# Moving the split weights' buffers in SBUF relative to the activations: a one-layer decoder on one core

## Chip, cores and metric

The kernel runs on one core of a Trainium2 chip. The metric is the device time of one execution in microseconds (us); the median of 3 runs is given, and a profile of one further execution.

## What is computed

One decoder layer over 512 tokens of width 1024, in float32. It has three parts, each followed by a layer norm of the sum with its input: a parallel mixer (chunked gMLP and stick-breaking attention behind one input projection, merged by gates, and an output projection), cross-attention into 256 memory tokens, and a mixture of 64 SwiGLU experts with 8 experts a token plus a shared one. Cut to what takes most of the time:

```python
proj = x @ w_in + b_in                               # 1024 x 7168
x = layer_norm(ALPHA * x + merged @ w_out)           # after gMLP and attention
m = softmax(q @ k.T) @ v @ w_mem_o                   # 4 heads, 256 memory tokens
moe = swiglu(x, w_sh_gate, w_sh_up, w_sh_down) + \
    routed_experts(x, idx, gate_w, w_exp_gate, w_exp_up, w_exp_down)   # 64 experts
```

## The kernel before, in words

**Products in three parts.** Each float32 operand of a large product is split into hi (rounded to fp32r) and lo (the rest, also fp32r). ScalarE writes hi and VectorE writes lo (`split`, line 80). A product is then three matmuls (`mm3`, lines 83 to 85): first operand's hi with the second's hi, hi with lo, lo with hi. The first argument pair of `mm3` holds the weights that are loaded into the array (128 x 128), the second is streamed through it (256 or 512 columns). While one matmul streams its operand, the weights of the next are loaded.

**Where the split weights lie.** `wpieces` (line 87) brings weight matrices from HBM through a ring of 1 MB slots and splits them in pieces of 1024 elements a partition into the pool `wq`. There, hi and lo have a tag each (`h` and `l`) with four buffers of 4096 bytes, so there are four pairs that are used in turn. The same pool takes the pieces of the shared expert's down projection (`shared`, line 637), of each expert's gate and up weights (`block_up`, line 712, two tiles for each half) and of its down weights (`down_split`, line 737, two tiles). Each pair serves two rows of K at 512 columns, which is six matmuls in the expert stage.

**Addresses.** A pool's tiles lie one behind the other in SBUF, and pools on the left side lie behind the pools opened earlier; some pools are placed from the right end. Worked out from the tiles' sizes, nearly all operands of TensorE start at 224 bytes modulo 512, and so do their slices: the eight buffers of `wq`, the activations `xTh`/`xTl`, the experts' `xb`, `hth` and `htl`, the attention's operands, `Mh`/`Ml`. Others are: the memory queries `QTh`/`QTl` and probabilities `PTh`/`PTl` at 64; the memory keys and `Vl` (right side) at 480; the shared expert's `HTh`/`HTl` at 32; the router's weights, whose slices are 256 bytes long, by turns at 224 and 480.

**Order of the work.** First the memory keys and values; then four pairs of attention heads, each with four projections (`proj_feat` streams the activations past the weights, `proj_tok` streams the weights past the activations); then the gMLP's v and u blocks, the gate, the output projection, memory attention, router, shared expert. The experts come last, 65 blocks (64 experts and one for an expert with over 128 tokens) of 128 rows each. In a block TensorE does 12 matmuls of the first half of gate and up, two transposes for the block before it, 12 of the second half, eight transposes of the gathered rows of the next block, and 12 of the down projection of the block before. Both halves and the down projection have 512 columns, with weights streamed past the activations. POOL gathers rows and adds results by indirect DMA; SP issues the weight loads.

```python
    def split(hi, lo, src):
        return nc.scalar.copy(hi, src), nc.vector.tensor_sub(lo, src, hi.bitcast(FT))

    def mm3(ps, s, m, start, stop):
        nc.tensor.matmul(ps, s[0], m[0], start=start, stop=False)
        nc.tensor.matmul(ps, s[0], m[1], start=False, stop=False)
        nc.tensor.matmul(ps, s[1], m[0], start=False, stop=stop)
```

```python
        for k0 in range(4 * half, 4 * half + 4, 2):
            hi = wq.tile([128, 2, 2, EH], FR, name="ehi", tag="h")
            lo = wq.tile([128, 2, 2, EH], FR, name="elo", tag="l")
            split(hi, lo, wgu[half][:, :, k0 - 4 * half:k0 - 4 * half + 2].rearrange("p g k n -> p k g n"))
            for j in range(2):
                k = k0 + j
                m = (hi[:, j].rearrange("p g n -> p (g n)"), lo[:, j].rearrange("p g n -> p (g n)"))
                mm3(hp, (x[:, k, 0], x[:, k, 1]), m, k == 0, k == KC - 1)
```

Of the kernel before, what the change touches and what calls it, by code (L numbers as in the profile page):

```python
# [10 lines left out]
FR = mybir.dt.float32r  # L11
# [8 lines left out]
D = 1024  # L20
# [6 lines left out]
EH = 256  # L27
# [11 lines left out]
def decoder_layer(ctx: ExitStack, tc: tile.TileContext, I, out, dbg=None):  # L39
# [4 lines left out]
    wq = ctx.enter_context(tc.tile_pool(name="wq", bufs=4, reuse_waits="tile"))  # L44
# [17 lines left out]
    def accps(i=None):  # L62
        return pp.tile([128, 512], FT, name="acc", tag="a", bufs=4)
# [9 lines left out]
    mhalf = cp.tile([128, 1], FT, name="mhalf")  # L73
    nc.vector.memset(mhalf, -0.5)

    def bcast(src, n):
        return bass.AP(tensor=src.tensor, offset=src.offset, ap=[[0, 128], [1, n]])

# [8 lines that stand above are left out]
    def wpieces(view, K, N):  # L87

        per = min(K, 2048 // N)
        kk = max(1, 1024 // N)  # L90
        raw = []
        for k0 in range(0, K, per):
            raw.append(ring.tile([128, per, N]))
            nc.sync.dma_start(raw[-1], view[:, k0:k0 + per])
        for k0, r in zip(range(0, K, per), raw):
            for k1 in range(0, per, kk):
                hi = wq.tile([128, kk, N], FR, name="whi", tag="h")
                lo = wq.tile([128, kk, N], FR, name="wlo", tag="l")
                split(hi, lo, r[:, k1:k1 + kk])
                for j in range(kk):  # L100
                    yield k0 + k1 + j, (hi[:, j], lo[:, j])

    def resident(view, K, N):
        return [w for _, w in wpieces(view, K, N)]

    def ln_load(g, b):
        gt, bt = row_pair("ln", "t01")
        nc.sync.dma_start(gt, bcast(g, D))
        nc.sync.dma_start(bt, bcast(b, D))
        return gt, bt  # L110
# [68 lines left out]
    with tc.tile_pool(name="pk", bufs=1, reuse_waits="tile") as pk:  # L179
# [8 lines left out]
        for c in range(2):  # L188
            on_act, on_dve = transpose_split(mth, mtl, mts[c], c)
        wk = wpieces(w_kv[:, :, 0:512], KC, 512)  # L190
        with tc.issue_after(on_act.ins), tc.issue_after(on_dve.ins):
            w0 = next(wk)
# [431 lines left out]
    for c in range(NCH):  # L624
        o = pps[:, c * NE:(c + 1) * NE]
# [11 lines left out]
    def shared():  # L637
        with tc.tile_pool(name="sh", bufs=1, reuse_waits="tile") as sh:
            HTh = sh.tile([128, 2, T], FR, name="HTh")
            HTl = sh.tile([128, 2, T], FR, name="HTl")  # L640
            wsg = resident(I["w_sh_gate"][0].rearrange("(p k) n -> p k n", k=KC), KC, EH)
            wsu = resident(I["w_sh_up"][0].rearrange("(p k) n -> p k n", k=KC), KC, EH)
            for hf in range(2):
                hs = slice(hf * 256, (hf + 1) * 256)
                for j in range(2):
                    js = slice(j * 128, (j + 1) * 128)
                    pg, pu = accps()[:, 0:256], accps()[:, 0:256]
                    for w, ps in ((wsg, pg), (wsu, pu)):
                        for k in range(KC):
                            mm3(ps, (w[k][0][:, js], w[k][1][:, js]), (xTh[:, k, hs], xTl[:, k, hs]),  # L650
                                k == 0, k == KC - 1)
                    SG = sh.tile([128, 256], FT, name="SG", tag="SG", bufs=2)
                    nc.scalar.activation(SG, pg, AF.Silu)
                    nc.vector.tensor_tensor(SG, SG, pu, op=OP.mult)
                    split(HTh[:, j, hs], HTl[:, j, hs], SG)
            stage = xp.tile([128, NCH, D], FT, name="stage", tag="xTh")
            wsd = ring.tile([128, 2, D])
            nc.sync.dma_start(wsd, I["w_sh_down"][0].rearrange("(k p) n -> p k n", p=128))
            for n0 in (0, 512):
                hi = wq.tile([128, 2, 512], FR, name="shi", tag="h")  # L660
                lo = wq.tile([128, 2, 512], FR, name="slo", tag="l")
                split(hi, lo, wsd[:, :, n0:n0 + 512])
                for c in range(NCH):
                    cs = slice(c * 128, (c + 1) * 128)
                    ps = accps()
                    for k in range(2):
                        mm3(ps, (HTh[:, k, cs], HTl[:, k, cs]), (hi[:, k], lo[:, k]), k == 0, k == 1)
                    nc.scalar.copy(stage[:, c, n0:n0 + 512], ps)
                    if n0:
                        nc.scalar.dma_start(accv[1][:, c], stage[:, c])  # L670
# [8 lines left out]
    for i in range(4):  # L679
        t = ea.tile([128, D], FT, name="xg%d" % i, tag="xg%d" % i, bufs=1)  # L680
# [31 lines left out]
    def block_up(wgu, slot, half, hp):  # L712

        x = late[1][:, slot]
        for k0 in range(4 * half, 4 * half + 4, 2):
            hi = wq.tile([128, 2, 2, EH], FR, name="ehi", tag="h")
            lo = wq.tile([128, 2, 2, EH], FR, name="elo", tag="l")
            split(hi, lo, wgu[half][:, :, k0 - 4 * half:k0 - 4 * half + 2].rearrange("p g k n -> p k g n"))
            for j in range(2):
                k = k0 + j  # L720
                m = (hi[:, j].rearrange("p g n -> p (g n)"), lo[:, j].rearrange("p g n -> p (g n)"))
                mm3(hp, (x[:, k, 0], x[:, k, 1]), m, k == 0, k == KC - 1)

    def block_h(hp, gate):
        hh = late[0].tile([128, EH], FT, name="hh", tag="hh")
        nc.scalar.activation(hh, hp[:, 0:EH], AF.Silu)
        mark[0] = nc.vector.scalar_tensor_tensor(hh, hp[:, EH:2 * EH], gate, hh, op0=OP.mult, op1=OP.mult)
        hv = hh.rearrange("t (p k) -> t k p", k=2)
        hps = zps().rearrange("p (k t) -> p k t", k=4)
        for k in range(2):  # L730
            nc.tensor.transpose(hps[:, k], hv[:, k], idf)  # L731
        hth = late[0].tile([128, 2, 128], FR, name="hth", tag="hth")
        htl = late[0].tile([128, 2, 128], FR, name="htl", tag="htl")
        split(hth, htl, hps[:, 0:2])
        return hth, htl

    def down_split(wd):
        w = []
        for k in range(2):
            hi = wq.tile([128, D], FR, name="dhi", tag="h")  # L740
            lo = wq.tile([128, D], FR, name="dlo", tag="l")
            split(hi, lo, wd[:, k])
            w.append((hi, lo))
        return w
# [134 lines left out]
    N = len(queue)  # L879
# [34 lines left out]
    for n in range(N):  # L914
# [5 lines left out]
        if prev:  # L920
            h = block_h(prev[1], prev[3])
# [97 lines left out]
```

## Time and profile before

| | |
|---|---|
| runs, median of 3 | 1233.82 us (1233.71 to 1235.24) |
| profiled execution | 1231.37 us |
| its span, first to last instruction | 1229.7 us |
| TensorE busy | 1172.8 us, 95% |
| VectorE busy | 958.5 us, 78% |
| ScalarE busy | 805.8 us, 66% |

A matmul's row tells when it starts and how long until its end; matmuls overlap, so what counts for a run of them is the distance from one start to the next. Lines 80 and 83 to 85 are those of helpers, so groups are told apart by their tiles: `ehi`, `elo` are the experts' gate and up weights, `dhi`, `dlo` their down weights, `whi`, `wlo` all weights that come through `wpieces`, `shi`, `slo` the shared expert's down weights. In a matmul's row the streamed operand and the weights stand behind the arrow, in either order.

### The profile page before, as it was taken

The page shows a single profiled execution, that of the slowest core. Times are in us where ns is not written, and L with a number is a line of the kernel's source. Part 1 is how long each engine was busy: PE and PEld are TensorE (multiplying, and loading weights), DVE is VectorE, ACT ScalarE, POOL GpSimd, SP SyncE. Part 2 cuts the span into 40 slices and gives each one's busy share as a digit, 9 for nine tenths or more (in the row PEclk, how much of TensorE's full clock was granted, in tenths as well). Part 3 has the DMA queues.
Part 4 walks back from the last instruction along what each step waited for, and adds up shares of the span by engine and source line. Part 5 has one row for each costly group of instructions (what it writes and reads, how often), then busy time and mean ns, then how long its engine had stood idle before and what let it go on. Part 6 is the DMA issues. An engine that isn't in the chain of part 4 may idle for free.

```text
span 1229.7 us, 17667 instructions
## 1 busy us (share of the span) xinstructions
PE 1172.8 (95%) x6301; PEld 992.5 (81%) x6301; DVE 958.5 (78%) x1427; ACT 805.8 (66%) x1198; POOL 267.4 (22%) x178
## 2 busy tenths in 40 slices
PE   7999999999999999989999999999999999999980
PEld 6887888878888889877888888888888888888860
DVE  6546556464745567885999999999999999999974
ACT  7444334343324346545888998989989899899971
POOL 2000000000200010121333433334433342334213
PEclk9999999999999999999999999999999999999995
DMA  9621322224333212477999999999999999999946
GB/s 342 215 85 57 107 69 70 69 69 141 117 106 135 103 62 102 171 265 268 360 393 376 385 397 370 379 368 394 389 383 389 383 385 371 368 374 340 388 115 150
DMA packets 102367, 307.73 MB, mean 250 GB/s; under 512 B 17358, under 2 KB 35334, under 8 KB 93446
## 3 DMA queue, kind: packets, MB, share of 16 engines
q1 hardware_dynamic: 78054, 259.05, 55.0%
q0 software_dynamic: 19296, 35.71, 12.1%
q10 hardware_dynamic: 4928, 11.83, 2.5%
q8 instruction: 50, 0.82, 0.3%
q14 instruction: 39, 0.32, 0.1%
HBM read 298.64 MB, written 42.47 MB: 277 GB/s over the span
## 4 chain that ended last, share of the span: by engine, by line
PE 77%; issue 6%; DVE 6%; DMA 5%; POOL 3%; ACT 1%; SPq 0%; POOLq 0%; DVEq 0%; ACTq 0%
PE acc L85 22%; PE acc L84 22%; PE acc L83 22%; PE trp L170 4%; DMA acc<-ys,idxs 2%; POOL acc L756 2%; DVE qq L283 2%; DMA ln<-in_ln_in_g_dram 1%; PE zp L84 1%; PE zp L85 1%; PE zp L83 1%; PE zp L731 1%; POOL xg L686 1%; DVE be L285 1%; DMA y<-acc 1%
## 5 line engine op out<-in xcount | busy, mean ns | idle before, releaser
L80 DVE TENSOR_TENSOR elo<-wraw,ehi 128x1024 fp32r<-128x1024 f32 x260 | 316.5, 1225 | 21.4 <-ACT ehi L80 20.4
L80 ACT CAST ehi<-wraw 128x1024 fp32r<-128x1024 f32 x260 | 274.1, 1055 | 44.4 <-PE acc L85 40.2
L83 PE MATMUL acc<-ehi,xb 128*128 128x512 f32 x520 | 208.1, 400 | 1.2 <-ACT xb L80 1.2
L85 PE MATMUL acc<-ehi,xb 128*128 128x512 f32 x520 | 205.9, 396 | 1.0 <-DVE xb L80 1.0
L84 PE MATMUL acc<-elo,xb 128*128 128x512 f32 x520 | 204.5, 393 | 0.0
L80 DVE TENSOR_TENSOR wlo<-wraw,whi 128x1024 fp32r<-128x1024 f32 x84 | 101.9, 1222 | 104.5 <-ACT whi L80 104.5
L80 ACT CAST whi<-wraw 128x1024 fp32r<-128x1024 f32 x84 | 87.5, 1050 | 127.4 <-PE acc L84 72.0
L756 POOL DMA_INDIRECT acc<-ys,idxs x65 | 130.9, 2014 | 170.4 <-ACT ys L755 145.0
L84 PE MATMUL acc<-xTl,whi 128*128 128x512 f32 (+1 forms) x448 | 162.0, 362 | 0.0
L83 PE MATMUL acc<-xTh,whi 128*128 128x512 f32 (+1 forms) x448 | 162.0, 362 | 0.0
L85 PE MATMUL acc<-xTh,wlo 128*128 128x512 f32 (+1 forms) x448 | 160.8, 360 | 0.0
L80 DVE TENSOR_TENSOR dlo<-wraw,dhi 128x1024 fp32r<-128x1024 f32 x130 | 156.2, 1218 | 0.6 <-ACT dhi L80 0.4
L686 POOL DMA_INDIRECT xg<-x2d,idxs x65 | 94.0, 1446 | 275.1 <-PE trp L170 228.9
L80 ACT CAST dhi<-wraw 128x1024 fp32r<-128x1024 f32 x130 | 137.4, 1057 | 18.0 <-PE acc L85 11.9
L85 PEld LDWEIGHTS acc<-ehi,xb 128*128 128x128 f32 x520 | 97.6, 188 | 21.5 <-DVE xb L80 1.6
L83 PEld LDWEIGHTS acc<-ehi,xb 128*128 128x128 f32 x520 | 98.4, 189 | 20.0 <-ACT xb L80 1.4
L84 PEld LDWEIGHTS acc<-elo,xb 128*128 128x128 f32 x520 | 97.9, 188 | 18.8
L83 PE MATMUL acc<-dhi,hth 128*128 128x512 f32 x260 | 106.8, 411 | 0.5 <-ACT hth L80 0.5
L85 PE MATMUL acc<-dhi,htl 128*128 128x512 f32 x260 | 102.3, 393 | 0.0
L84 PE MATMUL acc<-dlo,hth 128*128 128x512 f32 x260 | 102.1, 393 | 0.0
L83 PEld LDWEIGHTS acc<-xTh,whi 128*128 128x128 f32 x448 | 84.5, 189 | 12.2
L84 PEld LDWEIGHTS acc<-xTl,whi 128*128 128x128 f32 x448 | 84.6, 189 | 11.6
(270 smaller groups left out, 2126.3 us busy)
## 6 DMA issues: line engine op xcount, KB each, us to landing
wraw<-in_w_exp_gate_dram SPq DMA_DIRECT2D x130, 512.0 KB
wraw<-in_w_exp_up_dram SPq DMA_DIRECT2D x130, 512.0 KB
wraw<-in_w_exp_down_dram SPq DMA_DIRECT2D x65, 1024.0 KB
wraw<-in_w_in_dram SPq DMA_DIRECT2D x28, 1024.0 KB
wraw<-in_w_mem_kv_dram SPq DMA_DIRECT2D x4, 1024.0 KB
wraw<-in_w_out_dram SPq DMA_DIRECT2D x4, 1024.0 KB
X<-in_x_dram SPq DMA_DIRECT2D x4, 512.0 KB
wraw<-in_w_mem_q_dram SPq DMA_DIRECT2D x2, 1024.0 KB
```

The lines of the kernel that those rows point to most:

```text
L80: return nc.scalar.copy(hi, src), nc.vector.tensor_sub(lo, src, hi.bitcast(FT))
L83: nc.tensor.matmul(ps, s[0], m[0], start=start, stop=False)
L84: nc.tensor.matmul(ps, s[0], m[1], start=False, stop=False)
L85: nc.tensor.matmul(ps, s[1], m[0], start=False, stop=stop)
L170: nc.tensor.transpose(ps[:, k], sv[:, k0 + k], idf)
L283: nc.vector.tensor_tensor_scan(qq[:, 0:n][:, ::-1], sy[:, 1:n + 1][:, ::-1], ones.to_broadcast([128, n]), 1.0, op0=OP.mult, op1=OP.mult)
L285: nc.vector.tensor_tensor(be[:, 0:n], be[:, 0:n], qq[:, 0:n], op=OP.mult)
L686: nc.gpsimd.indirect_dma_start(out=xg, out_offset=None, in_=x2d, in_offset=bass.IndirectOffsetOnAxis(ap=idx, axis=0), bounds_check=T - 1, ...
L731: nc.tensor.transpose(hps[:, k], hv[:, k], idf)
L756: nc.gpsimd.indirect_dma_start(out=accs[acc], out_offset=bass.IndirectOffsetOnAxis(ap=idx, axis=0), in_=ys, in_offset=None, bounds_check=T ...
```

## The change

The four pairs get a tag each (`p0` to `p3`) with one buffer that holds hi and lo, lo 4096 bytes behind hi. In front of hi lie 16, 32, 192 and 64 bytes; the tiles have 8224, 8224, 8384 and 8256 bytes, 33,088 in all where the eight buffers had 32,768. So every tile behind the pool on the left side moves by 320 bytes, the activations from 224 to 32 modulo 512, and the pairs lie at 240, 288, 480 and 32. Relative to the activations that is 208, 256, 448 and 0. `QTh` and `PTh` come to 384, `HTh` to 352; tiles on the right side stay. A function `wpair` hands out the pairs in turn, and all four places that took buffers of `wq` call it. The instructions, their order and the transfers are the same.

```diff
+    taken = [0]
+
+    def wpair(shape, name):
+
+        i = taken[0] % 4
+        taken[0] += 1
+        off = (4, 8, 48, 16)[i]
+        t = wq.tile([128, off + 4 * (i == 0) + 2048], FR, name=name + "ABCD"[i], tag="p%d" % i, bufs=1)
+        sub = dict(zip("abc", shape))
+        names = " ".join(sub)
+        return [t[:, o:o + 1024].rearrange("p (%s) -> p %s" % (names, names), **sub)
+                for o in (off, off + 1024)]
+
...
-                hi = wq.tile([128, kk, N], FR, name="whi", tag="h")
-                lo = wq.tile([128, kk, N], FR, name="wlo", tag="l")
+                hi, lo = wpair([kk, N], "whi")
...
-                hi = wq.tile([128, 2, 512], FR, name="shi", tag="h")
-                lo = wq.tile([128, 2, 512], FR, name="slo", tag="l")
+                hi, lo = wpair([2, 512], "shi")
...
-            hi = wq.tile([128, 2, 2, EH], FR, name="ehi", tag="h")
-            lo = wq.tile([128, 2, 2, EH], FR, name="elo", tag="l")
+            hi, lo = wpair([2, 2, EH], "ehi")
...
-            hi = wq.tile([128, D], FR, name="dhi", tag="h")
-            lo = wq.tile([128, D], FR, name="dlo", tag="l")
+            hi, lo = wpair([D], "dhi")
```

## Rows read from the trace of the kernel before

**Rows 1.** The page, part 1: busy us, share of the span, instructions.
```profile
PE 1172.8 (95%) x6301; PEld 992.5 (81%) x6301; DVE 958.5 (78%) x1427; ACT 805.8 (66%) x1198; POOL 267.4 (22%) x178
```

**Rows 2.** Busy time by stage; columns as in the first line.
```profile
core 0: us, PE busy (x) PEld busy (x) DVE busy (x) ACT busy (x) POOL busy (x), PEclk, DMA share, GB/s
...
42.00:354.00 312.00, 308.10 (x1612) 259.08 (x1611) 167.29 (x301) 115.95 (x199) 9.24 (x12) 1.00 0.29 96
354.00:460.00 106.00, 105.14 (x521) 88.23 (x520) 64.52 (x98) 41.91 (x55) 5.39 (x5) 1.00 0.27 93
460.00:519.00 59.00, 59.00 (x406) 54.18 (x406) 47.53 (x113) 33.73 (x78) 5.12 (x4) 1.00 0.36 125
...
572.00:1184.00 612.00, 609.23 (x3167) 510.04 (x3168) 590.24 (x706) 548.44 (x767) 215.41 (x124) 1.00 1.00 369
```

**Rows 3.** The page, part 4: the chain that ended last, by line.
```profile
PE acc L85 22%; PE acc L84 22%; PE acc L83 22%; PE trp L170 4%; DMA acc<-ys,idxs 2%; POOL acc L756 2%; DVE qq L283 2%; DMA ln<-in_ln_in_g_dram 1%; PE zp L84 1%; PE zp L85 1%; PE zp L83 1%; PE zp L731 1%; POOL xg L686 1%; DVE be L285 1%; DMA y<-acc 1%
```

**Rows 4.** Waits from 650 to 1100 us: us in total, times, longest.
```profile
ACT ehi L80 <- PE acc L85: 29.0, 91, 0.5
...
DVE elo L80 <- ACT ehi L80: 5.3, 29, 0.3
```

**Rows 5.** Timeline of TensorE, gMLP stage: start us, us; first and last of 103 matmuls.
```profile
328.27 0.39 PE L83 MATMUL acc<-xTh,whi 128*128 128x512 f32 x1
...
351.39 0.39 PE L83 MATMUL acc<-xTh,whi 128*128 128x512 f32 x1
```

**Rows 6.** Timeline of TensorE in one expert, its runs' ends.
```profile
845.84 1.05 PE L170 MATMUL trp<-idf,xg 128*128 128x128 f32 x8
...
852.38 0.48 PE L83 MATMUL acc<-ehi,xb 128*128 128x512 f32 x1
852.69 0.40 PE L84 MATMUL acc<-elo,xb 128*128 128x512 f32 x1
...
855.00 0.40 PE L85 MATMUL acc<-ehi,xb 128*128 128x512 f32 x1
855.24 1.05 PE L170 MATMUL trp<-idf,xg 128*128 128x128 f32 x8
856.05 0.48 PE L83 MATMUL acc<-dhi,hth 128*128 128x512 f32 x1
856.37 0.40 PE L84 MATMUL acc<-dlo,hth 128*128 128x512 f32 x1
...
861.39 0.40 PE L85 MATMUL acc<-ehi,xb 128*128 128x512 f32 x1
861.63 0.39 PE L731 MATMUL zp<-idf,hh 128*128 128x128 f32 x2
```

**Rows 7.** Timeline, shared expert's down projection (offset 192), first and last of 48.
```profile
559.72 0.40 PE L83 MATMUL acc<-shi,HTh 128*128 128x512 f32 x1
...
570.69 0.40 PE L85 MATMUL acc<-shi,HTl 128*128 128x512 f32 x1
```

**Rows 8.** Timeline, memory output projection (offset 160), first and last of 15.
```profile
515.08 0.40 PE L83 MATMUL acc<-whi,QTh 128*128 128x512 f32 x1
...
518.36 0.40 PE L85 MATMUL acc<-whi,QTl 128*128 128x512 f32 x1
```

**Rows 9.** Timeline, memory queries: 256 columns, offset 0, first and last of 13.
```profile
480.98 0.28 PE L85 MATMUL acc<-xTh,wlo 128*128 128x256 f32 x1
...
482.42 0.28 PE L85 MATMUL acc<-xTh,wlo 128*128 128x256 f32 x1
```

**Rows 10.** Timeline, memory attention: offset 416 (two places), then 352 and 96.
```profile
474.34 0.28 PE L84 MATMUL zp<-KTl,QTh 128*128 128x256 f32 x1
...
474.92 0.29 PE L83 MATMUL acc<-xTh,whi 128*128 128x256 f32 x1
...
477.80 0.28 PE L83 MATMUL acc<-PTh,Vh 128*128 128x256 f32 x1
...
478.39 0.29 PE L85 MATMUL acc<-PTh,Vl 128*128 128x256 f32 x1
...
479.08 0.28 PE L84 MATMUL zp<-KTl,QTh 128*128 128x256 f32 x1
...
479.66 0.29 PE L83 MATMUL acc<-xTh,whi 128*128 128x256 f32 x1
```

**Rows 11.** Timeline, router: each third matmul, offsets 0 and 256 by turns.
```profile
520.67 0.28 PE L83 MATMUL zp<-xTh,wroh 128*64 128x256 f32 x1
...
521.01 0.28 PE L83 MATMUL zp<-xTh,wroh 128*64 128x256 f32 x1
...
521.35 0.28 PE L83 MATMUL zp<-xTh,wroh 128*64 128x256 f32 x1
```

**Rows 12.** Groups by form, activations streamed: count, busy us, mean ns, idle before.
```profile
L83 PE MATMUL acc<-xTh,whi 128*128 128x512 f32 x320 | 125.4, 393 | 0.0
```

**Rows 13.** Waits of the whole span.
```profile
ACT whi L80 <- PE acc L84: 72.0, 22, 5.8
```

**Rows 14.** Groups by form, VectorE's subtraction into tiles at 224 and 64.
```profile
L80 DVE TENSOR_TENSOR xTl<-trp,xTh 128x512 fp32r<-128x512 f32 x24 | 15.6, 682 | 2.0 <-ACT xTh L80 2.0
...
L80 DVE TENSOR_TENSOR PTl<-trp,PTh 128x512 fp32r<-128x512 f32 x8 | 5.5, 685 | 0.5 <-ACT PTh L80 0.5
```

## Prediction

> **What bounds the kernel now.** I read the page's engine totals first, then the busy time by stage, the chain that ended last, the waits inside the expert stage, and last the start times of single matmuls. TensorE is busy 95% of the span [rows 1]. [...] Its matmuls carry the chain too: three lines with 22% each [rows 3]. Between 650 and 1100 us nobody on the matrix path waits for a transfer; ScalarE waits for TensorE, 29.0 us in all [rows 4]. So the time is the number of matmuls times the distance between their starts. VectorE stands next: 590.24 of 612 us among the experts [rows 2]. If TensorE's part there shrank by more than about 3.6%, VectorE would be the bound.
>
> The distance is not one number. "Offset" below means the address of the streamed operand minus that of the next matmul's weights, modulo 512 bytes, worked out from the tile sizes. At offset 0 a long run of 512-column matmuls takes 23.12 us for 102 starts: 226.7 ns each, settled [rows 5]. One expert shows runs that don't begin so. Behind each group of transposes a run starts slowly: in a run of twelve, the starts from the second matmul to the twelfth lie 2.31 us apart for 10 distances (231.0 ns); a run of 24 gets to the settled distance, 5.02 us for 22 (228.2 ns) [rows 6]. With the last matmul of each run (0.24 us, twice) that is 7.81 us for 34 distances, 229.7 ns on average; the two first matmuls behind transposes (0.32 us) wait for their weights and stay. The same pattern stands in every expert I looked at, whatever ScalarE and VectorE do meanwhile, so it belongs to TensorE's own two reads.
>
> Where the operands lie at another offset, the distance is another one. At 192 bytes, the shared expert's down projection, 47 starts take 10.97 us: 233.4 ns, and it never settles [rows 7]. At 160 bytes, the memory output projection, 14 take 3.28 us: 234.3 ns [rows 8]. At 256 columns offset 0 gives 1.44 us for 12, 120.0 ns [rows 9]; offset 416 gives 0.58 us for 5 in two places, about 117 ns, and a mix of 352 and 96 gives 0.59 us for 5, 118 ns [rows 10]. In the router (64 weight columns) groups of three alternate between offsets 0 and 256, and each group takes 0.34 us [rows 11].
>
> **The change part by part.** It adds no instruction and removes none; it moves operands. Weights streamed past activations get offsets 208, 256, 448, 0 from pair to pair; where the activations stream past the weights they are 304, 256, 64, 0. A pair serves six matmuls in the expert stage, then the next pair comes. I price each offset against the settled 226.7 ns by its nearest row.
>
> - Weights streamed: 208 is nearest to 192, +6.7 ns. 256 has its own rows in the router, 0, though with half the weight columns. 448 is nearest to 416, -3 ns. Offset 0 is 0. The mean is +0.9, so 227.6 ns.
> - Activations streamed: 304 is nearest to 352, -2; 256: 0; 64 is nearest to 96, -2; 0: 0. The mean is -1.0.
> - Experts: 65 of them with 34 distances are 2,210; 227.6 - 229.7 = -2.1 ns each: -4.6 us.
> - Earlier stages with activations streamed: three lines of 320 [rows 12], 960 matmuls, -1.0 ns: -1.0 us. With weights streamed 384 (two blocks of the gMLP value and the output projection): +0.9 ns, +0.3 us.
> - Memory output projection, some 95 matmuls: offsets become 368, 416, 96 and 160, on average 226.9 ns for 233 to 234 now: -0.6 us. Shared down projection, 48 matmuls, offsets 352 bytes less than its pair's place, near 400 to 448: -3 for +6.7 now, -0.5 us.
> - The 256-column matmuls of the projections, some 800: offsets of both signs, taken as 0.
>
> Sum: -4.6 - 1.0 + 0.3 - 0.6 - 0.5 = -6.4 us. The bounds come from the same rows: if every offset gave -3 ns, the experts would give 6.0 x 2,210 = 13.3 us, the earlier 1,344 matmuls 4.0, the 256-column ones 2.4, with the last two terms 21 us; if all stood at 234.3 ns, the experts would lose 4.6 x 2,210 = 10.2 us and the earlier ones 7.6 x 1,344 = 10.2, 20 us in all.
>
> Three edits cost nothing. **The shared tile**: buffers now come free when both parts are read, so ScalarE's next hi waits for the lo's last reader, one matmul (0.23 us) later where it used to wait for line 84 [rows 13]; four pairs cover it, as TensorE sat idle 0.0 us before these matmuls [rows 12]. Without that cover it would be 84 tiles x 0.23 = 19 us. That readers of hi should now wait for the writer of lo is unlikely: xb already holds both in one tile, and line 83 and line 85 wait for different engines there. **The splits' alignment**: VectorE's 512-element subtraction takes 682 ns into a tile at 224 bytes modulo 512 and 685 into one at 64 [rows 14]; no row starts at 240, as pair A will. Ten ns on a quarter of the splits would be about 1 us, on an engine that has 3.6% to spare. **The shift of everything behind the pool by 320 bytes**: it leaves those tiles' offsets to each other; only tiles on the right side change theirs (the memory keys from 416 to 96), under 100 short matmuls, taken as 0.
>
> **The rivals.** (1) *The settled rhythm is lost, slower.* The place is the distance after a switch. Only offset 0 ever reached 226.7 ns; both other offsets at 512 columns never did in 47 and 14 starts [rows 7, 8], and after a break it takes offset 0 about ten matmuls [rows 6], while a pair now lasts six. With three pairs at 233.4 and the fourth at 231.0 the mean is 232.8 ns: the experts lose 3.1 x 2,210 = 6.9 us, the earlier 1,344 matmuls 6.1 ns each, 8.2 us, less 0.6 for the two small stages: +14.5 us, 1248.3 us. It decides from the point where the experts' mean passes 229.7 ns. Against it: the 256-column rows, where three other offsets are shorter than 0. (2) *Nothing moves.* The two slow 512-column places differ from the rest in more than the offset (other tiles, short stages), and the router's groups don't differ at all. Then the time stays, 1233.8 us. [...] (3) *All offsets but 0 help,* as at 256 columns, and the repeated slow start goes as well: the lower bound, -21 us, 1213 us. VectorE would still leave room for its 13.3 us (2.2% of 612).
>
> **How the numbers follow.** The profiled execution took 1231.37 us (its span 1229.7, 1.7 around it), 2.4 below the median of the runs, 1233.82. The sum puts it at 1225.0, the median at 1227.4; I say 1227.4. About 0.2%, 2.5 us, is what a measurement of this kernel can tell from no change. Chances: the forecast 0.40, rival 3 0.07, both faster: 0.47. Rival 2, with what of the forecast falls within 2.5 us of no change, 0.17. Rival 1 0.36: its rows have the right width and two of them agree, while the forecast leans on rows of half that width. The range reaches from rival 3 to a little beyond rival 1: 1213 to 1251.
>
> **What would show it.** In the changed profile, start times of matmuls within one expert, pair by pair: 233 ns on the pair at 208, near 227 on those at 256 and 0, near 224 on 448. The long runs of the first 460 us near 226 ns. The period of an expert, now 9.40 us from one group of eight transposes to the next, at 9.33. ScalarE's waits for TensorE may grow, and VectorE's share of the expert stage should rise to 97%. I am wrong if the distances change but their mean in an expert lies above 229.7 ns, if the expert's matmuls begin to wait for VectorE where they waited for ScalarE, or if the distances stay as they are.

## The result, and the profile after

The change is slower: 1244.96 us median of 4 runs (1244.48 to 1248.62) against 1234.53 us for the kernel before in the same batch, ratio 1.0097, 95% interval 1.0083 to 1.011. (The ratios of this document are the record's estimates over all executions; the quotient of these two medians is 1.0084.) The forecast was 1227.4 us, faster. The profiled execution took 1248.62 us, the longest of the four, and its span is 1246.9 us; its granted clock was on average 0.982 of the full one, that of the other three 0.985 or 0.986, so its rows are read by stage and not as a total.

The page, part 1, of the kernel after (busy us, share of the span, instructions) answers to [rows 1]:

```profile
PE 1184.0 (95%) x6301; PEld 994.6 (80%) x6301; DVE 962.0 (77%) x1427; ACT 806.6 (65%) x1198; POOL 257.9 (21%) x178
```

TensorE has the same 6301 instructions and 11.2 us more busy time. Busy time by stage of the kernel after, with the cuts and columns of [rows 2]:

```profile
42.00:354.00 312.00, 306.41 (x1595) 255.82 (x1594) 170.24 (x302) 116.92 (x200) 9.24 (x12) 1.00 0.29 95
354.00:460.00 106.00, 105.38 (x498) 86.89 (x497) 59.28 (x87) 36.94 (x48) 3.28 (x3) 1.00 0.29 100
...
572.00:1184.00 612.00, 609.23 (x3133) 504.90 (x3133) 578.47 (x690) 539.32 (x753) 203.06 (x122) 1.00 1.01 373
```

Among the experts TensorE is busy for the same 609.23 us but starts 3133 matmuls where it started 3167, at the same clock. It is as full as before and each matmul takes longer. VectorE's share fell to 94.5%, so it is not the new bound. The chain that ended last has not moved either, against [rows 3]:

```profile
PE acc L96 23%; PE acc L98 23%; PE acc L97 23%; PE trp L182 4%; DMA acc<-ys,idxs 2%; POOL acc L765 1%; DVE qq L295 1%; PE zp L741 1%; PE zp L97 1%; PE zp L96 1%; PE zp L98 1%; POOL xg L697 1%; DMA wraw<-in_w_mem_kv_dram 1%; DVE be L297 1%; DMA y<-acc 1%
```

The timeline of TensorE in one expert after the change (start us, us), where the pairs now have names, answers to [rows 6]:

```profile
855.80 0.40 PE L97 MATMUL acc<-ehiC,xb 128*128 128x512 f32 x1
...
858.35 1.05 PE L182 MATMUL trp<-idf,xg 128*128 128x128 f32 x8
859.16 0.48 PE L96 MATMUL acc<-dhiA,hth 128*128 128x512 f32 x1
859.48 0.40 PE L97 MATMUL acc<-dhiA,hth 128*128 128x512 f32 x1
...
860.65 0.39 PE L96 MATMUL acc<-dhiB,hth 128*128 128x512 f32 x1
...
862.01 0.39 PE L96 MATMUL acc<-ehiC,xb 128*128 128x512 f32 x1
...
863.41 0.39 PE L96 MATMUL acc<-ehiD,xb 128*128 128x512 f32 x1
...
864.56 0.40 PE L98 MATMUL acc<-ehiD,xb 128*128 128x512 f32 x1
```

Read it by differences. Pair A at offset 208: 1.17 us for 5 starts, 234 ns. Pair B at 256: 1.36 us for 6, 226.7 ns. Pair C at 448: 1.40 us for 6, 233.3 ns. Pair D at 0, right behind C: 1.15 us for 5, 230 ns, so here offset 0 has not settled. Over all experts (means of the distances at 512 columns from 572 to 1190 us, of trace start times; e1 is a run from below, with the change's tiles and all pairs at offset 0):

```
pair            A        B        C        D       mean
offset          208      256      448      0
priced          233.4    226.7    223.7    226.7
after           234.3    229.1    233.4    230.4   231.8
e1, all at 0    230.1    228.3    229.9    228.0   229.1
before          229.0 for all (offset 0)           229.0
```

A run behind transposes always begins with A or C, so B and D meet the slow start only at its end: that is why they are the faster ones in e1. After the change they are slower than there, although their own offsets are good: they now come behind a pair at 208 or 448 and, but for the place of the rows above where B has 226.7 ns at once, do not settle at once: from the first start in a pair on, the distances in the experts are on average 230, 231, 231, 226 and 228 ns in B and 227, 235, 229, 233 and 230 in D. From one group of eight transposes to the next an expert now takes 9.48 or 9.49 us by turns instead of 9.40, some 5 us over all of them. That is only half of the loss. A part of the rest shows at the very start. The timeline of ScalarE in the kernel before, from 5 us on:

```profile
5.84 0.59 ACT L80 CAST mth<-trp 128x512 fp32r<-128x512 f32 x1 [3.76 <-PE trp L170]
...
9.70 4.00 ACT L80 CAST whi<-wraw 128x1024 fp32r<-128x1024 f32 x4
```

and in the kernel after, with TensorE's rows around its first weights below, and TensorE's first product with weights in the kernel before last:

```profile
9.01 1.05 ACT L93 CAST whiB<-wraw 128x1024 fp32r<-128x1024 f32 x1 [6.93 <-DMA wraw<-in_w_mem_kv_dram]
9.96 1.06 ACT L93 CAST mth<-trp 128x512 fp32r<-128x512 f32 x2
11.71 1.05 ACT L93 CAST whiC<-wraw 128x1024 fp32r<-128x1024 f32 x1 [0.69 <-DMA wraw<-in_w_mem_kv_dram]
12.66 1.04 ACT L93 CAST whiD<-wraw 128x1024 fp32r<-128x1024 f32 x1
13.61 1.06 ACT L93 CAST mth<-trp 128x512 fp32r<-128x512 f32 x2
14.57 1.05 ACT L93 CAST whiA<-wraw 128x1024 fp32r<-128x1024 f32 x1
```

```profile
11.97 1.97 PE L182 MATMUL trp<-idf,mt 128*128 128x128 f32 x8 [5.50 <-DVE mtl L93]
15.67 0.58 PE L96 MATMUL acc<-mth,whiA 128*128 128x256 f32 x1 [1.74 <-ACT whiA L93]
```

```profile
10.80 0.38 PE L83 MATMUL acc<-mth,whi 128*128 128x256 f32 x1 [1.62 <-ACT whi L80]
```

The order of ScalarE's work is another one. Before, the copies of the transposed memory come first and the four splits of weights after them. Now the split of pair B stands at the head of the queue and waits 6.93 us for its weights, with the copy that TensorE's next transposes need behind it; and the split of pair A, the first that TensorE uses, comes last of the four. The first product with weights starts at 15.67 us; in the kernel before it starts at 10.80. The sentence ahead of the prediction that the order of the instructions stays the same was wrong. The build orders each engine's instructions itself, and with other buffer names it chose another order; e4 below shows that the names alone do this. The source holds the first split of weights behind the memory's transposes with an `issue_after`, and it does so for that one split alone. While all hi buffers were one name with four buffers, the next splits stayed behind the first; with a name each they pass it.

### The profile page after: what moved, and what is told of

It reads as the page before. It is cut to its first block, busy times and chain, and to the rows that moved or that the text cites. A ratio compares the mean times of both kernels' runs of the same rounds, so it can differ in the third digit from the quotient of the medians.

```text
span 1246.9 us, 17656 instructions
## 1 busy us (share of the span) xinstructions
PE 1184.0 (95%) x6301; PEld 994.6 (80%) x6301; DVE 962.0 (77%) x1427; ACT 806.6 (65%) x1198; POOL 257.9 (21%) x178
## 4 chain that ended last, share of the span: by engine, by line
PE 78%; issue 8%; DVE 5%; DMA 4%; POOL 3%; ACT 2%; POOLq 0%; SPq 0%; DVEq 0%; ACTq 0%
PE acc L96 23%; PE acc L98 23%; PE acc L97 23%; PE trp L182 4%; DMA acc<-ys,idxs 2%; POOL acc L765 1%; DVE qq L295 1%; PE zp L741 1%; PE zp L97 1%; PE zp L96 1%; PE zp L98 1%; POOL xg L697 1%; DMA wraw<-in_w_mem_kv_dram 1%; DVE be L297 1%; DMA y<-acc 1%
## 5 line engine op out<-in xcount | busy, mean ns | idle before, releaser
L93 DVE TENSOR_TENSOR ehiB<-wraw,ehiB 128x1024 fp32r<-128x1024 f32 x65 | 80.2, 1234 | 8.7 <-ACT ehiB L93 8.6
L93 DVE TENSOR_TENSOR xb<-trp,xb 128x512 fp32r<-128x512 f32 x130 | 83.4, 681 | 4.0 <-ACT xb L93 3.3
L93 DVE TENSOR_TENSOR ehiD<-wraw,ehiD 128x1024 fp32r<-128x1024 f32 x65 | 80.7, 1242 | 6.6 <-ACT ehiD L93 6.0
L93 DVE TENSOR_TENSOR ehiA<-wraw,ehiA 128x1024 fp32r<-128x1024 f32 x65 | 79.1, 1217 | 5.3 <-ACT ehiA L93 5.0
L93 DVE TENSOR_TENSOR ehiC<-wraw,ehiC 128x1024 fp32r<-128x1024 f32 x65 | 79.2, 1219 | 3.3 <-ACT ehiC L93 2.8
L93 ACT CAST ehiB<-wraw 128x1024 fp32r<-128x1024 f32 x65 | 68.8, 1058 | 10.6 <-PE acc L98 7.8
L93 ACT CAST xb<-trp 128x512 fp32r<-128x512 f32 x130 | 69.6, 586 | 1.6 <-PE trp L182 1.6
L182 PE MATMUL trp<-idf,xg 128*128 128x128 f32 x520 | 68.8, 274 | 0.0
L96 PE MATMUL acc<-ehiC,xb 128*128 128x512 f32 x130 | 54.2, 417 | 1.2 <-ACT xb L93 1.2
L96 PE MATMUL acc<-ehiA,xb 128*128 128x512 f32 x130 | 54.1, 416 | 0.0
L98 PE MATMUL acc<-ehiC,xb 128*128 128x512 f32 x130 | 51.6, 397 | 1.1 <-DVE xb L93 1.1
L97 PE MATMUL acc<-ehiA,xb 128*128 128x512 f32 x130 | 52.3, 402 | 0.0
```

The costliest lines, as they stand in the source:

```text
L182: nc.tensor.transpose(ps[:, k], sv[:, k0 + k], idf)
```

## The experiments

The theory after reading the result was that the offset sets the distance, with wrong prices for 448, 304 and 64. The rivals were that the switch from pair to pair does it, that another engine's accesses do it, and that sharing the tile costs the time. **m1_offsets** is a kernel of its own: runs of 32 matmuls at each offset and nothing else; the rest of the layer is left out.

```diff
+    def run(name, m0, n, offs, wcols=128):
+        for r, o in enumerate(offs):
+            ps = acc[r % 2][0:wcols, 0:n]
+            for j in range(RUN):
+                w = 4096 + o + 256 * (j % 4)
+                nc.tensor.matmul(ps, big[:, w:w + wcols], big[:, m0:m0 + n],
+                                 start=j == 0, stop=j == RUN - 1)
```

> This kernel leaves the layer out: it only runs 32 matmuls in a row at each of 32 offsets (512 and 256 streamed columns, 128 weight columns; also streams that start 16 or 32 bytes further with their weights, and 64 weight columns), with no other engine at work. Theory 1 (the offset of stream and weights modulo 512 alone sets the settled distance): at 512 columns about 226.7 ns at 0 and 256, 233.4 at 192, 234.3 at 160 and 208, 233.3 at 448, 232 to 233 at 304, about 230 at 64, and the same when both operands start 32 bytes further. Theory 2 (the longer distances of the changed kernel come from changing from pair to pair): all offsets settle near 226.7 ns here. Theory 3 (other engines' accesses to the same memory make the difference): all offsets alike here, below 226 ns.

Mean of the last 16 distances of each run, ns, by stream address minus weight address modulo 512, worked out from start times:

```
512 columns: 226.7 at 0 (227.3 in the kernel's first run), 16, 240, 256, 272, 496; 230.0 at 80, 336; 231.9 at 176, 432;
             233.3 to 233.6 at 32 to 64, 96 to 144, 192 to 224, 288 to 320, 352 to 400, 448 to 480;
             234.1 at 160, 416
256 columns: 120.0 at 0, 16, 256, 272; 113.3 at 192, 448; 116.7 at 32, 48, 288, 304;
             117.7 to 120 elsewhere
64 weight columns, 256 streamed: 113.3 at 0 and 256, 116.6 to 119 elsewhere
```

31 matmuls in a row at 512 columns, offset 256 and then 448, and the same two offsets at 256 columns, from the timeline of m1:

```profile
137.24 7.19 PE L35 MATMUL a<-big 128*128 128x512 f32 x31
```

```profile
47.96 7.39 PE L35 MATMUL a<-big 128*128 128x512 f32 x31
```

```profile
316.43 3.88 PE L35 MATMUL a<-big 128*128 128x256 f32 x31
```

```profile
271.03 3.68 PE L35 MATMUL a<-big 128*128 128x256 f32 x31
```

So the addresses make the difference, with no other engine at work and no change of offset on the way, and in this series the pattern repeats after 256 bytes. The offset is not all of it, as theory 1 of m1 had it: with both operands 32 bytes further 64 has 228.7 ns, not 233.3, and with both 16 bytes further 0 has 231.1, 256 has 233.4 and 64, 160 and 224 have 226.7. At 512 columns nothing is faster than the 226.7 ns of offset 0. At 256 columns the picture is nearly turned round: 448 is the best offset there, with 192, and 0 among the worst. With 64 weight columns 0 and 256 are alike and both the best, which is why the router's groups did not differ [rows 11].

**e1_all0, e2_all448 and e3_all256** keep the change's four shared tiles and give all pairs one offset:

```diff
-        off = (4, 8, 48, 16)[i]
-        t = wq.tile([128, off + 4 * (i == 0) + 2048], FR, name=name + "ABCD"[i], tag="p%d" % i, bufs=1)
+        off, tail = (0, 0, 0, 0)[i], (0, 0, 0, 0)[i]
+        t = wq.tile([128, off + tail + 2048], FR, name=name + "ABCD"[i], tag="p%d" % i, bufs=1)
```

with a tail of 16 elements behind the last pair for 448 and of 64 for 256.

> hi and lo share a tile as in the change, but all four pairs stay at offset 0. Theory 1 (offsets): the time of before, 1234.5 us within 0.2%, and expert matmuls 229.7 ns apart. Rival (the shared tile, which is freed later, costs the time): 1245 us as after the change.

> All four pairs at offset 448. Theory 1 (offsets): expert matmuls 233.3 ns apart throughout instead of 231.8 on average after the change, activations streamed at 64 about 230 ns; 1246 to 1250 us. Theory 2 (changing from pair to pair costs): one offset throughout settles, so 1234.5 us.

> All four pairs at offset 256. Theory 1 (offsets): 256 settles at 226.7 ns as 0 does, so the time of before within 0.3%, 1231 to 1238 us. Theory 2 (changing from pair to pair costs): 1234.5 us too; this run tells theory 1 from the view that any offset but 0 is longer, which gives over 1243 us.

Offset 0 took 1239.79 us (ratio to before 1.004, 1.0026 to 1.0054), 256 took 1239.78 (1.0039, 1.0026 to 1.0051), 448 took 1246.77 (1.0101, 1.0074 to 1.0128). The timeline of the kernel with 448, pairs C and D of one expert:

```profile
858.52 0.39 PE L96 MATMUL acc<-ehiC,xb 128*128 128x512 f32 x1
...
859.92 0.39 PE L96 MATMUL acc<-ehiD,xb 128*128 128x512 f32 x1
...
861.09 0.40 PE L98 MATMUL acc<-ehiD,xb 128*128 128x512 f32 x1
```

11 starts in 2.57 us, 233.6 ns, from end to end. At 0 and 256 the experts' mean is 229.06 ns, as before. So 448 costs 6.7 ns over the settled distance and 256 nothing, with no switching in play. Switching costs something besides. In the kernel with offset 0 for all, pair D right behind C:

```profile
860.37 0.39 PE L96 MATMUL acc<-ehiD,xb 128*128 128x512 f32 x1
...
861.50 0.40 PE L98 MATMUL acc<-ehiD,xb 128*128 128x512 f32 x1
```

Five distances take 1.13 us, 226 ns, where the change had 1.15 us behind its slow pair C. The kernel at 256 was expected at 1231 to 1238 us and lies above, and of the two sides expected for offset 0, 1234.5 and 1245, neither came: offset 0 with the shared tile is still 5 us slower than before, with experts that run at the old distance. Something outside the experts costs those 5 us. The next runs split the loss.

**e4_own_tags** puts hi and lo back into tiles of their own at offset 0, each of the eight with a name of its own; **e5_one_tag** keeps the shared tile at offset 0, but as four buffers of one name.

```diff
 e4
+        parts = [(wq.tile([128, 1024], FR, name=name[:-2] + part + "ABCD"[i], tag="%s%d" % (part, i), bufs=1), 0)
+                 for part in ("hi", "lo")]
 e5
+        t = wq.tile([128, 2048], FR, name=name, tag="p", bufs=4)
+        parts = ((t, 0), (t, 1024))
```

> Offset 0 for all; hi and lo in tiles of their own as in the kernel before, but each of the eight buffers with its own name in the pool, taken in turn. In the build this changes only the order around the start: the second split of weights comes ahead of the copies of the transposed memory on ScalarE, and the first split, for which TensorE waits, comes last of the four. Theory A (the loss of the shared-tile kernels has two parts, the start and the sharing): the first stage loses 5 us by matmul 50 and keeps 2 to 3 of it, 1235.5 to 1237. Rival B (sharing the tile is all of it): 1233.6. Rival C (the order at the start is all of it): 1238.5. The experts keep 229.0 ns in every case.

> Offset 0 for all; hi and lo share a tile, but the four tiles are buffers of one name, so the start keeps the order of before; the order of ScalarE's and VectorE's work between the heads differs from before, as in the change. Theory A (two parts): 1236 to 1237.5, nothing lost by matmul 200, 2 to 3 us lost between matmul 200 and 3400. Rival B (sharing is all): 1238.5. Rival C (the start is all): 1233.6. Experts 229.0 ns.

e4 took 1238.05 us (ratio 1.0027, 1.0015 to 1.004), e5 1236.41 (1.0027, 1.0016 to 1.0038): two parts of about 3.3 us each, as theory A had it. e4's median lies above theory A's 1237 and near the 1238.5 of rival C (by the ratio it stands at 1237.0), but rival C has nothing lost in e5 and rival B nothing in e4, and the two intervals rule both out. The sum of the two, 1.0054, lies at the upper end of e1's interval (1.004, 1.0026 to 1.0054). TensorE's rows in e4 repeat the start of the kernel after:

```profile
11.83 1.97 PE L182 MATMUL trp<-idf,mt 128*128 128x128 f32 x8 [5.24 <-DVE mtl L93]
15.52 0.58 PE L96 MATMUL acc<-mth,whiA 128*128 128x256 f32 x1 [1.72 <-ACT whiA L93]
```

In e5 ScalarE has the old start again, four splits behind the copies:

```profile
9.21 0.59 ACT L91 CAST mth<-trp 128x512 fp32r<-128x512 f32 x1 [0.27 <-PE trp L180]
9.70 4.07 ACT L91 CAST whi<-wraw 128x1024 fp32r<-128x1024 f32 x4
```

What e5 loses, it loses mostly between the heads, where the order of the splits among the softmax work differs, and TensorE's own order with it. TensorE's waits from 42 to 240 us (us in total, times, longest), kernel before and then e5:

```profile
PE trp L288 <- DVE sy L282: 2.1, 6, 0.4
PE trp L288 <- DVE be L285: 0.5, 3, 0.2
```

```profile
PE trp L298 <- DVE be L295: 2.7, 6, 0.7
PE trp L298 <- DVE sy L292: 1.3, 3, 0.5
```

That is 1.4 us more waiting of the transposes for VectorE, under half of e5's 3.3; the rest is spread. e5 has the other order and the later release of a shared tile together, and no run parts the two.

**e7_offsets_alone** has the offsets without the order: hi and lo apart, the first four splits all held behind the memory's transposes, offsets 192, 256, 448 and 0 (192 instead of 208). Every engine's list of instructions is that of the kernel before.

```diff
+        off = (0, 16, 48, 16)[i]
+        parts = [(wq.tile([128, lead + 1024], FR, name=name[:-2] + part + "ABCD"[i], tag="%s%d" % (part, i), bufs=1), lead)
+                 for part, lead in (("hi", off), ("lo", 0))]
...
+        def held(pieces):
+            while True:
+                with tc.issue_after(on_act.ins), tc.issue_after(on_dve.ins):
+                    piece = next(pieces, None)
+                if piece is None:
+                    return
+                yield piece
```

> Offsets 192, 256, 448 and 0 for the four pairs, hi and lo in tiles of their own, and the order of every engine's work as in the kernel before. Theory (offsets and order add up): the change's 1244.96 less the 1239.79 of the shared tile at offset 0 is 5.2, less 0.9 between the two batches' medians of before and 0.4 for 192 in place of 208: about 1237.5 here, 1237 to 1238.5. In the experts pair A 233.3 ns, pair C 233.3, B and D 229 or less. Rival (order is all that counts, TensorE's longer distances are covered): 1233.6. Rival (the two multiply: slow matmuls hide behind the worse order's waits in the change): 1241 or more.

1239.34 us, ratio 1.0041 (1.0026 to 1.0056); the experts' means are 233.5 (192), 230.4 (256), 233.4 (448) and 230.4 (0). The theory's 1237 to 1238.5 lay low, but its side holds: the three parts, 0.27%, 0.27% and 0.41%, add up to 0.95% of the time, and the change loses 0.97%. Each part is known to 0.11 to 0.15%, so it is luck that the two come so close; with e1's 0.40% for names and sharing together the sum is 0.81%. Where each part arises, by the start of the matmul behind the first n in the profiled executions, us:

```
n                      50      200      2000     2800     3400     6300
before                16.76    43.39   391.17   532.46   633.15  1194.38
names (e4)            21.50    45.57   393.37   534.54   638.79  1200.05
shared tile (e5)      16.76    44.58   394.84   535.94   637.51  1198.76
offsets (e7)          16.47    44.86   393.38   534.54   635.83  1202.00
after                 22.16    46.16   398.07   539.31   643.90  1209.76
```

The names cost 4.7 us by the 50th matmul, and 2.6 of it come back, as TensorE pauses in the kernel before anyway (busy for 4.03 of the 6 us from 22 to 28). The offsets cost 4.9 of their 7.6 us behind the 3400th matmul, among the experts.

Not all of the table is the edits' work: the granted clock has a part. The stretch from 2800 to 3400 took between 100.7 us (before) and 104.8 us (e1). The columns of [rows 2] for it, in the kernel before, e5, e4 and the kernel after:

```profile
532.46:633.15 100.69, 96.54 (x602) 83.73 (x601) 82.50 (x161) 67.43 (x98) 25.68 (x16) 0.99 0.88 316
```

```profile
535.94:637.51 101.57, 97.32 (x602) 83.77 (x601) 82.68 (x165) 67.46 (x98) 25.66 (x16) 0.98 0.89 319
```

```profile
534.54:638.79 104.25, 100.11 (x602) 86.61 (x601) 82.84 (x165) 67.87 (x98) 24.81 (x16) 0.95 0.86 309
```

```profile
539.31:643.90 104.59, 100.37 (x603) 86.41 (x602) 83.08 (x165) 67.62 (x98) 22.77 (x16) 0.95 0.87 310
```

In the nine profiled kernels the granted clock stood at 0.5 of the full one for between 2.3 us (before) and 11.5 us (e1) of this stretch, and the stretch less half of that time is 99.0 to 100.2 us in all of them. So the 3.6 us that e4 loses here, and the 3.9 of the kernel after, are time at the halved clock; in the profiled execution of e4 the order itself costs about 2.1 us, what it has lost by the 2800th matmul. Why the clock fell more often in some of the kernels is open. e4's executions took 1234.67 to 1235.86 us where their mean clock was 0.985 or 0.986, and 1237.91 to 1240.84 where it was 0.981 to 0.983, so its 0.27% holds both. The same goes for the 1.2 and 1.5 us of e5 and e7 by the 200th matmul. From 28 to 45 us, the kernel before and e5 (e7 has the same 0.90):

```profile
28.00:45.00 17.00, 16.85 (x86) 14.14 (x86) 15.71 (x22) 11.99 (x17) 1.52 (x1) 1.00 0.83 268
```

```profile
28.00:45.00 17.00, 17.00 (x80) 14.40 (x80) 14.93 (x22) 12.09 (x17) 1.52 (x1) 0.90 0.76 246
```

That left the 229.0 ns of the experts themselves, 2.3 over the settled distance. **m2_block** is TensorE's part of an expert alone, at six offsets and with four places of the identity that the transposes stream; **m3_identity** stays at offset 0 and tries 18 places; at the first, 128, the build put all transposes ahead of the matmuls, so 17 count. The code of m3 (m2 has the offset in place of the first 0 and its own places for `idf`):

```diff
+        idf = ids[:, e:e + 128]
...
+            mms(0, 12, acc[0])
+            for k in range(2):
+                nc.tensor.transpose(zp[:, k * 128:k * 128 + 128], flat[:, 1048 + k:1048 + k + 256:2], idf)
+            mms(0, 12, acc[0])
+            for k in range(8):
+                q = (k % 4) * 128
+                nc.tensor.transpose(trp[:, q:q + 128], flat[:, 2088 + k:2088 + k + 1024:8], idf)
+            mms(0, 12, acc[1])
```

> Only TensorE's part of an expert block, with nothing else running: 12 matmuls of 512 columns, two transposes, 12, eight transposes, 12, four times over at each of the offsets 0, 16, 32, 208, 224, 240 and with the identity at four places; all else of the layer is left out. Theory (how soon the distance settles after transposes depends on the offset): at 0 some 8 of the 11 distances behind the transposes lie above 228, as in the kernel before, about 71 ns a block over 226.7 each; at 240 they are 226.7 from the second on, at 16 slower than at 0; 32, 208 and 224 lie at 233. Rival (the transposes leave a state that every offset needs as long to leave): the same excess at 0, 16 and 240. Rival (in the kernel before other engines make the slow ones): no excess at 0 here.

Part of the theory fell. Neither 240 nor 16 keeps its 226.7 ns in blocks with transposes: behind the first matmul of each run 16 gives means of 231.3 ns, 240 of 235 to 236, and its blocks are on average the longest of the six offsets at every place of the identity. What stands is the slow start at offset 0: with the identity where the kernel has it, the distances behind the two transposes are 233, 236, 224, 231, 236, 228, 233, 231, 226, 227 ns with nothing else running, and in the kernel before the run that starts at 852.38 [rows 6] has the same ten. No other engine makes them. And the place of the identity mattered, so:

> Only TensorE's part of an expert block at offset 0, five times over for each of 18 places of the identity that the transposes stream (every 16 bytes from 128 to 368, then 448 and 64 modulo 512); all else of the layer is left out. The look before had 9,400 ns a block at 128, 9,360 at 192, 9,407 at 256 and 9,367 at 320. Theory (the place of the identity against the transposed operand and the weights behind it sets at which point of the rhythm the run behind the transposes starts, and it repeats after 256 bytes as the offsets do): 448 gives 9,360 as 192 does, 64 gives 9,367 as 320 does, and some place lies at 9,330 or below, 11 distances settled within three. Rival (the four times of the look before differ by what came before the block): 192 and 448, 64 and 320 differ by as much as neighbours do.

The timeline of m2 with the identity at 128, and of m3 with it at 192:

```profile
722.89 0.39 PE L48 MATMUL zp<-ids,raw 128*128 128x128 f32 x2
723.03 3.02 PE L40 MATMUL a<-big 128*128 128x512 f32 x12
725.90 1.05 PE L52 MATMUL trp<-ids,raw 128*128 128x128 f32 x8
726.70 5.75 PE L40 MATMUL a<-big 128*128 128x512 f32 x24
732.29 0.39 PE L48 MATMUL zp<-ids,raw 128*128 128x128 f32 x2
```

```profile
209.71 0.40 PE L46 MATMUL zp<-ids,raw 128*128 128x128 f32 x2
209.86 2.99 PE L38 MATMUL a<-big 128*128 128x512 f32 x12
...
219.07 0.40 PE L46 MATMUL zp<-ids,raw 128*128 128x128 f32 x2
```

From one pair of transposes to the next a block takes 9.40 us at 128 and 9.36 at 192; the twelve matmuls behind the pair take 2.99 us in all, where m2 has 3.02. The blocks take 9,360 ns at 192, 304 and 448, 9,366 at 320 and 64, 9,407 at 224 and 256, and something between at the other places (176 has 9,357 and 9,376 by turns). Where it was tried, for 192 and 448 and for 64 and 320, the pattern repeats after 256 bytes here too. No place gave 9,330, as the theory had hoped.

**e8_identity** takes this to the kernel before: the identity moves by 64 bytes, the rest of the left side by 256.

```diff
-    idf = cp.tile([128, 128], FT, name="idf")
+    idf = cp.tile([128, 192], FT, name="idf")[:, 16:144]
```

> The kernel before with the identity 64 bytes further modulo 256 against everything else on the left side; order and offsets of all matmuls of 512 columns as before. Theory (the block alone decides: 9,400 ns with the identity at 128, 9,360 at 192): 40 ns less in each of 65 expert blocks, 2.6 us, so 1230 where before has 1232.6, or 1231 where it has 1233.65; the mean distance in the experts falls from 229.06 by 40/34, to 227.9 ns, and about 11 distances of a block lie over 228 where 16 do. Transposes of the earlier stages can add or take up to 1 us. Rival (the experts are paced by another engine or by the weights' loads once TensorE gains 40 ns): the distances behind the transposes fall as in the block, gaps appear elsewhere, and the time stays within 0.5 us.

1230.41 us against 1233.53, ratio 0.9979 (0.997 to 0.9988): faster than both kernels. The timeline of one expert:

```profile
852.61 0.39 PE L731 MATMUL zp<-idf,hh 128*128 128x128 f32 x2
852.76 0.48 PE L83 MATMUL acc<-ehi,xb 128*128 128x512 f32 x1
853.07 0.40 PE L84 MATMUL acc<-elo,xb 128*128 128x512 f32 x1
...
855.35 0.40 PE L85 MATMUL acc<-ehi,xb 128*128 128x512 f32 x1
```

The run of twelve behind the two transposes takes 2.28 us from the second start to the twelfth, where [rows 6] had 2.31. The experts' mean distance is 227.98 ns (227.9 was expected), 24% of the distances lie over 228 instead of 39%, and the period is 9.36 us. The gain arises among the experts: from the 3400th matmul to the 6300th e8 takes 559.1 us, the kernel before 561.2.

## Why the prediction was wrong

**The bound was right.** TensorE's distances set the time of the long stages before and after (609.23 of 612 us busy among the experts in both), and the instruction count (6301), the chain (three lines of 22%, then of 23%) and the granted clock of the expert stage (1.00) did not move. That the distance hangs on the offset is shown by m1 with nothing else running: 226.7 ns at 0 and 233.3 at 448, at 512 columns.

**208 and 256 were priced right.** 208 from its neighbour 192 came to 234.3 ns in place of 233.4; 256 settles at 226.7 ns as 0 does (m1, e3).

**448, 304 and 64 failed, and with them the sign.** The step was to price them, at 512 columns, by rows of 256 columns [rows 10]. For 448 that row had the right sign at its width: m1 has 113.3 ns at 448 and 118.8 at 416 against 120.0 at 0. But the gain does not carry over: at 512 columns 448 costs 6.7 ns where the sum had -3. Nearness in offset was given more weight than sameness of shape, while a row of the right width, [rows 7], was at hand; as m1's pattern at 512 columns repeats after 256 bytes, its 192 even has the price of 448 (233.3 to 233.6 ns for both). With +6.7 for 448, the mean of the four prices is 3.35 ns instead of 0.9, and the experts' term becomes 230.05 - 229.7 = +0.35 ns, +0.8 us instead of -4.6. The activations' two prices, 304 and 64, were -2 each, from 352 and 96, which m1 has at 119.9 ns even at 256 columns, no gain at all; the trace has 232.6 and 230.6 ns against 227.1 at 0 (42 to 460 us). The two small stages were to gain 1.1 us by moving to better offsets. There are none: the memory output projection's 368, 416, 96 and 160 have 233 to 234 ns in m1, and of the shared down projection's four offsets two are not near 400 to 448 but at 128 and 192; all four have 233.

**The slow starts were taken away for nothing.** The same term set prices on the settled 226.7 ns against a mean of before, 229.7, that has the slow starts behind transposes in it. The change does not remove them. A and C, which stand behind the transposes, now have 234.3 and 233.4 ns on average where e1 has 230.1 and 229.9, and a slow start comes behind them, when B or D begins: 229.1 and 230.4 ns, where 226.7 was put and where the same matmuls have 228.3 and 228.0 with all pairs at 0. That is the rest of the experts' loss: the trace's mean is 231.8 against 229.0 by the same count, +2.8 ns, not +0.35. It is also the first of the prediction's own signs of being wrong, a mean above that of before.

**The shared tile was costed at 0, and about half of the loss lies there.** The prediction priced the later release of a buffer and named its cover. What it did not see is that buffer names and tile sharing are an input to the order in which the build issues the work. e4 and e5 put 0.27% on the names and 0.27% on the sharing, e1 0.40% on both; a part of that is the clock in the stretch from 2800 to 3400. The cover named for it, four pairs and an idle time of 0.0 us, was read in the long stages; the places that paid were the first 20 us, where no four pairs are ahead (4.7 us by the 50th matmul in e4), and the heads, where the splits share ScalarE and VectorE with the softmax (in e5 the transposes wait 1.4 us more for VectorE from 42 to 240 us). How much of e5's part is the order and how much the later release is not shown.

**The rivals.** Rival 1 had the right sign and half of the mechanism: two of its three offsets do stay at 233 to 234 ns, and the settled rhythm is lost behind them (229.1 and 230.4 ns on B and D), but 256 settles at 226.7 ns like 0 (m1). That its number, 1248.3 us, lies near the result is luck: it put 14.5 us on the offsets, which alone cost 0.41%, 5.1 us (e7), and it knew nothing of the order. Rival 2 fell with the first trace. Rival 3 fell with m1: no offset is better at 512 columns than the 226.7 ns of 0. The range, 1213 to 1251, held the result, because rival 1 stood at its upper end.

## What to carry to other kernels

Price an operand's address by rows of the same shape or measure it alone, since here 448 had, with 192, the shortest distance at 256 columns (113.3 ns, 120.0 at 0) and a long one at 512 (233.3, 226.7 at 0). A change of buffer names or of sharing reordered the engines' work here though no instruction was added (TensorE's first product with weights moved from 10.80 to 15.52 us by the names alone, e4), so compare the order of instructions before arguing that a tile change costs nothing. When only part of a rewrite helps, put its parts back one at a time: here offsets, names and sharing cost about 0.41%, 0.27% and 0.27% and were summed in one number. And before a difference between two profiles is put down to an edit, compare the granted clock of the same stretch: one stretch differed here by 4 us from that alone.

## What the runs showed of the hardware

- At 512 streamed columns and 128 weight columns the distance between matmuls repeated with the offset after 256 bytes in m1's first series: 226.7 ns within 16 bytes of 0 or 256, 230 to 234 ns elsewhere. The absolute place had a say too: with stream and weights 16 bytes further, 226.7 ns stood at 64, 160, 224, 320, 416 and 480, 231.1 at 0 and 233.4 at 256.
- Behind six matmuls at 448 a pair at offset 0 did not settle within its five distances in the change: 1.15 us for the five distances of pair D behind C in one expert, 1.13 behind a pair at 0 (e1); over all experts 230.4 ns against 228.0.
- At 256 columns the distance was shortest, 113.3 ns, at 192 and 448, and 120.0 at 0 (m1).
- Offset 240 gave 226.7 ns in runs of 32 (m1) and 235 to 236 in the runs between transposes (m2).
- The address of the operand that the transposes stream changed the speed of the matmuls behind them: 9,360 to 9,407 ns a block (m3), and 0.21% of the kernel's time, 2.6 us (e8).
- Between the 2800th and the 3400th matmul the granted clock stood at 0.5 of the full one for 2.3 to 11.5 us in the nine profiled kernels, and the stretch took 100.7 to 104.8 us with it.
- With no other engine at work, m1 had 226.7 ns at offset 0 and 233.3 at 448, at 512 columns: the addresses of the two operands alone made the difference.
